# Seven block products for eight in the down projection of a two-layer encoder

## The chip, the cores and the metric

The kernel runs on one core of one Trainium2 chip. The metric is the device time of one execution in microseconds (us), lower being better. Five engines work side by side: TensorE (PE) multiplies, with its weight loads shown as PEld; VectorE (DVE), ScalarE (ACT) and GpSimd (POOL) work on elements; SyncE (SP) issues most of the transfers (DMA). TensorE writes its results into eight banks of PSUM, each 128 rows by 512 float32 columns.

## The reference, cut to what matters

Two encoder layers over 512 tokens of width 1024, each a token mixer with an output projection and then a SwiGLU feed-forward block with D_FF = 2816. Only the feed-forward block is touched:

```
def _swiglu(h, w_gate_up, w_down):
    gu = h @ w_gate_up
    g, u = gu[..., :D_FF], gu[..., D_FF:]
    return (jax.nn.silu(g) * u) @ w_down
...
x = x + _swiglu(_rmsnorm(x, norm_ffn[i]), w_gate_up[i], w_down[i])
```

The last product, the down projection, multiplies a 512 x 2816 activation by a 2816 x 1024 weight matrix and adds the result to x.

## The kernel before

**Products in three passes.** Every float32 operand is split into a rounded high part and the rest (`whi` and `wlo` for weights, `ah`/`al` or the two halves of an `op` tile for activations). `mm3` (lines 135 to 139) issues three matmuls for each product of a 128x128 block by a 128x512 block: high by high, high by low, low by high. `wsplit` (line 151) makes the split of a 128x1024 weight tile: ScalarE copies the high part (L154), VectorE subtracts (L155). `split` (line 248) does the same for activations (L249, L250).

**Gate and up projection** (`ffn`, line 784). These are already done with seven products for eight (`PROD`, line 781): the rows of the activation fall into two halves of 256 tokens, the inner dimension into two halves, and gate and up are the two column halves. Six groups `g` of columns each run the seven products. A product is cut into weight tiles (the `steps` list, line 833); `ahead` prepares the tiles up to `LW` = 2 steps before TensorE needs them. Sums of weight tiles are made partly by VectorE (lines 814, 821, 824) and partly by transfers that GpSimd issues and that add onto a tile already in SBUF (`dma_add`, line 806). The operand sums of the activation are built once, in group 0 (`sums`, line 709), and kept. The products gather in the pairs of banks A, B, C and D (`BANK`, line 919), and `post` (line 883) adds them up. The pool behind `whi` and `wlo` has three buffers of each (`WF` = 3), the pool of raw weight tiles three (`RF` = 3), and a general pool "G" 33 tiles of 128x1024. The pool "T" has nine tiles of 128x512.

**Down projection** (lines 949 to 1000). The activation stands transposed in eleven tiles `AT[kp]`, each with two of the 22 row blocks of the inner dimension for all 512 tokens. For each half `c` of the 1024 output columns, and each of the eleven `kp`, one weight tile is loaded and split, and 24 matmuls follow (four groups of 128 tokens, two row blocks, three passes). `split_a` (line 958) splits the activation tiles once, and both halves use the split. Four banks hold a half; `add_x` adds them to x (L686; in layer 1 line 998, after which line 999 writes the output). The transposes for the next layer (`emit(0)`, `emit(1)`) stand inside the second half and behind it, and `emit("weights")` loads the next layer's first two weight tiles early.

**Order of work.** The program text gives each engine's instructions a priority; a scheduler at build time fixes the order on each engine. On the chip every engine runs its own list in that order.

Of the kernel before, what the change touches and what calls it, by code (L numbers as in the profile page):

```python
# [18 lines left out]
P = 128  # L19
S = 512  # L20
D = 1024
# [27 lines left out]
def encoder_kernel(ctx: ExitStack, tc: tile.TileContext, a: dict, out: bass.AP):  # L49
# [14 lines left out]
    def wtile(dt, tag, bufs=None):  # L64
        return wpool[0][1].tile([P, wpool[0][2]], dt, tag=tag, name=nm(tag), **({"bufs": bufs} if bufs else {}))
# [10 lines left out]
    def g4(shape=(P, 1024), dt=F32R, name="g"):  # L76
        return gp_.tile(list(shape), dt, tag="G", name=nm(name))
# [25 lines left out]
    def bank(tag):  # L103
        return ps.tile([P, 512], F32, tag=tag, name=nm(tag), bufs=CFG[tag])

    def small(n, tag, dt=F32, bufs=4):
        return sp.tile([P, 1 if n == 1 else 16], dt, tag=tag, name=nm(tag), bufs=bufs)[:, :n]

    def f(ap):
        return ap.bitcast(F32)  # L110
# [32 lines left out]
    def eng(kind):  # L143
        c = cnt.get(kind, 0)
        cnt[kind] = c + 1
        p = CFG[kind]
        return p[c % len(p)]

    phase = ["s"]

    def wsplit(raw, n, kind):

        hi, lo = wtile(F32R, "whi"), wtile(F32R, "wlo")
        A.copy(hi[:, :n], raw)  # L154
        (V if eng(kind) == "V" else GP).tensor_sub(lo[:, :n], raw, f(hi[:, :n]))  # L155
        return hi, lo
# [12 lines left out]
    def load_w(src, n):  # L169
        return wsplit(load_raw(src, n)[:, :n], n, "wlo" + phase[0])  # L170
# [509 lines left out]
        transposes(tb, [X[t][:, k * P : (k + 1) * P] for t in range(4)])  # L680
        return tb

    def add_x(X, c, bs, sq, ts=range(4)):
        for t in ts:
            xc = X[t][:, c * 512 : (c + 1) * 512]
            V.tensor_add(xc, bs[t], xc)  # L686
            A.activation(tt(), xc, AF.Square, accum_out=sq[:, 4 * c + t : 4 * c + t + 1])

    def w_out(l, acts, banks, pre, X, g0, first, early):
# [94 lines left out]
    def ffn(l, X, acts, banks, pre, g0, emit):  # L784


        phase[0] = "f"
        NG = 6
        raws = {}
        ops = {}  # L790
        AT = {}
# [4 lines left out]
        def ntile(g):  # L796
            return 2 if g < 5 else 1
# [33 lines left out]
            return w  # L831

        steps = [(g, p, i) for g in range(NG) for p in PROD for i in range(ntile(g))]
        ready = {}
        nprep = [0]

        def ahead(n):
            while nprep[0] < min(n, len(steps)):
                g, p, i = steps[nprep[0]]
                if g == i == 0:  # L840
                    ops[p] = getop[0](AOP[p])
                if i == 0:
                    for q in {"P1": [1, 3], "P7": [2]}.get(p, []):
                        load_q(g, q)
                    if p == "P6":
                        load_q(g + 1, 0)
                    if p == "P3":
                        load_q(g + 1, 1)
                ready[g, p, i] = prep(g, p, i)
                nprep[0] += 1  # L850
# [22 lines left out]
        def act_T(g, act):  # L873
            n = width(g)
            for j in range(n // P):
                fb = 4 * g + j
                if fb % 2 == 0:
                    AT[fb // 2] = g4((P, 2, 512), F32, "at")
                tb = bank("tp")
                transposes(tb, [act[t][:, j * P : (j + 1) * P] for t in range(4)])  # L880
                A.copy(AT[fb // 2][:, fb % 2], tb)  # L881
# [35 lines left out]
                return [st["p1"][0], st["p1"][1], st["p5"][0], st["p5"][1]]  # L917

        BANK = dict(P1="A", P7="B", P2="A", P5="C", P6="D", P4="B", P3="C")
        pend = None  # L920
        s = 0
        for g in range(NG):
# [23 lines left out]
                    pend = None  # L946
            pend = act

        sq = small(8, f"sd{l}", bufs=1)
        ws = {}  # L950

        def load_d(c, kp):
            if kp < NF // 2:
                ws[c, kp] = load_w(a["w_dn"][l, c, kp], 1024)

        asp = {}

        def split_a(kp):
            if kp < NF // 2 and kp not in asp:
                hi, lo = g4(name="ah"), g4(name="al")  # L960
                x = AT[kp].rearrange("p a b -> p (a b)")
                A.copy(hi, x)
                (V if eng("wlod") == "V" else GP).tensor_sub(lo, x, f(hi))
                asp[kp] = (hi, lo)

        for kp in range(2):
            split_a(kp)
            load_d(0, kp)
        act_T(NG - 1, pend)
        for c in range(2):  # L970
            bs = [bank(x) for x in ("mm", "sc", "mm", "sc")]
            for kp in range(NF // 2):
                split_a(kp + 2)
                if (c, kp) not in ws:
                    load_d(c, kp)
                hi, lo = ws.pop((c, kp))
                ah, al = asp[kp]
                for t in range(4):
                    for j in range(2):
                        cs_ = slice(j * 512 + t * P, j * 512 + (t + 1) * P)  # L980
                        mm3(bs[t], (ah[:, cs_], al[:, cs_]), (hi[:, j * 512 : (j + 1) * 512], lo[:, j * 512 : (j + 1) * 512]),
                            kp == j == 0, kp == NF // 2 - 1 and j == 1)
                if c == 0 and kp + 2 < NF // 2 and (c, kp + 2) not in ws:
                    load_d(c, kp + 2)
                elif c == 1 and kp + 1 < NF // 2:
                    load_d(c, kp + 1)
                if c == 1 and kp == 2:
                    emit(0)
                if c == 1 and kp == NF // 2 - 2:
                    emit("weights")  # L990
            if c == 0:
                load_d(1, 0)
            if l == 0:
                add_x(X, c, bs, sq)
            else:
                for t in range(4):
                    xc = X[t][:, c * 512 : (c + 1) * 512]
                    V.tensor_add(xc, bs[t], xc)
                    nc.sync.dma_start(out[t * P : (t + 1) * P, c * 512 : (c + 1) * 512], xc)
        emit(1)  # L1000
        phase[0] = "a"
        if l == 0:
            tot = small(4, "sqt")
# [455 lines left out]
def _layout(i):  # L1459
    x, mem = i["x"][0], i["mem"][0]  # L1460
    arr = {}
    arr["xT"] = x.T.reshape(NK, P, S)
    arr["memT"] = _pk(np.ascontiguousarray(mem.T), NK)[0]
    qn, kn = i["mla_q_norm"][0], i["mla_k_norm"][0]
    arr["gains"] = np.concatenate(
        [_cols(i["mem_norm"]), _cols(i["norm_mix"][0]), _cols(i["norm_mix"][1]),
         _cols(i["norm_ffn"][0]), _cols(i["norm_ffn"][1]),
         i["memq_norm"].T, i["memk_norm"].T, _cols(qn[:P]), _cols(kn[:P]),
         _cols(i["mla_q_a_norm"][0]), _cols(i["mla_kv_a_norm"][0])], 1)
    gq, gk = i["gqa_q_norm"][0], i["gqa_k_norm"][0]  # L1470
# [13 lines left out]
    w = i["mla_w_kv_b"][0].reshape(256, 4, 2, 2, P)  # L1484
    arr["w_kvb"] = np.stack([_pk(w[:, g].transpose(0, 2, 1, 3).reshape(256, 512), 2)[0] for g in range(4)])
    w = i["w_mem_kv"]
    arr["w_mkv"] = np.stack([np.stack([_pk(w[l, :, c * 512 : (c + 1) * 512], NK)[0] for c in range(2)]) for l in range(2)])
    arr["x"] = x.reshape(4, P, D)
    w = i["w_out"]
    arr["w_out"] = w.reshape(2, 6, 2, P, 2, 512).transpose(0, 4, 1, 3, 2, 5).reshape(2, 2, 6, P, 1024)  # L1490
    w = i["w_gate_up"].reshape(2, 2, 4, P, 2, DFF)
    m = w[..., :2560].reshape(2, 2, 2, 2, P, 2, 5, 512)
    arr["w_gu"] = m.transpose(0, 6, 1, 5, 2, 4, 3, 7).reshape(2, 5, 4, 2, P, 1024)
    arr["w_gl"] = w[..., 2560:].transpose(0, 1, 4, 3, 2, 5).reshape(2, 4, P, 1024)
    w = i["w_down"].reshape(2, NF // 2, 2, P, 2, 512)
    arr["w_dn"] = w.transpose(0, 4, 1, 3, 2, 5).reshape(2, 2, NF // 2, P, 1024)
    w = i["gqa_w_in"][0]
    arr["w_gin"] = np.stack([_pk(w[:, c : c + 512], NK)[0] for c in (1024, 1536, 0, 512)])
    return {k: np.ascontiguousarray(v) for k, v in arr.items()}

# [18 lines left out]
```

## Time and profile before

| what | us |
|---|---|
| median of 3 runs | 1275.64 |
| lowest and highest | 1274.54, 1277.09 |
| the profiled execution, its own time | 1276.39 |
| its span in the trace | 1274.6 |

The times are device times of whole executions. The span runs from the first to the last instruction that the profiler recorded, and is a little shorter than the execution's own time. The down projection of layer 0 runs from about 538 to 661 us of the span, that of layer 1 from about 1150 us to the end.

### The profile page before, as it was taken

The page shows a single profiled execution, that of the slowest core. Times are in us where ns is not written, and L with a number is a line of the kernel's source. Part 1 is how long each engine was busy: PE and PEld are TensorE (multiplying, and loading weights), DVE is VectorE, ACT ScalarE, POOL GpSimd, SP SyncE. Part 2 cuts the span into 40 slices and gives each one's busy share as a digit, 9 for nine tenths or more (in the row PEclk, how much of TensorE's full clock was granted, in tenths as well). Part 3 has the DMA queues.
Part 4 walks back from the last instruction along what each step waited for, and adds up shares of the span by engine and source line. Part 5 has one row for each costly group of instructions (what it writes and reads, how often), then busy time and mean ns, then how long its engine had stood idle before and what let it go on. Part 6 is the DMA issues. An engine that isn't in the chain of part 4 may idle for free.

```text
span 1274.6 us, 17121 instructions
## 1 busy us (share of the span) xinstructions
PE 1262.3 (99%) x6425; PEld 1060.2 (83%) x6425; DVE 906.7 (71%) x1634; ACT 701.1 (55%) x1205; POOL 28.7 (2%) x43
## 2 busy tenths in 40 slices
PE   9999999999999999999999999999999999999998
PEld 7988878988778888988888888888877888898887
DVE  6699999745987887853336798965488897786222
ACT  6587766845655555542233578866475555555110
POOL 1000000001000000000000000000100000000000
PEclk9999999999999999999999999999999999999999
DMA  6342101056355433342223212213626534336210
GB/s 236 113 143 86 36 1 67 1 215 165 98 151 165 127 105 100 114 151 66 80 89 113 79 64 67 83 67 116 170 63 197 165 75 141 100 92 223 61 55 33
DMA packets 49202, 136.07 MB, mean 107 GB/s; under 512 B 5680, under 2 KB 10288, under 8 KB 49120
## 3 DMA queue, kind: packets, MB, share of 16 engines
q1 hardware_dynamic: 44784, 119.58, 27.2%
q0 software_dynamic: 4336, 15.40, 6.8%
q8 instruction: 50, 0.82, 0.3%
q14 instruction: 32, 0.26, 0.1%
HBM read 132.87 MB, written 2.10 MB: 106 GB/s over the span
## 4 chain that ended last, share of the span: by engine, by line
PE 94%; DVE 3%; ACT 2%; DMA 0%; issue 0%; SPq 0%
PE mm L138 15%; PE mm L139 15%; PE mm L137 15%; PE sc L138 13%; PE sc L137 13%; PE sc L139 13%; PE tp L347 6%; PE sc L500 4%; DVE wlo L155 1%; ACT whi L154 1%; PE tp L566 1%; DMA raw<-in_w_cin 0%; ACT t L888 0%; DVE g L246 0%; ACT at L881 0%
## 5 line engine op out<-in xcount | busy, mean ns | idle before, releaser
L155 DVE TENSOR_TENSOR wlo<-raw,whi 128x1024 fp32r<-128x1024 f32 (+3 forms) x342 | 344.2, 1012 | 248.9 <-ACT whi L154 246.1
L154 ACT CAST whi<-raw 128x1024 fp32r<-128x1024 f32 (+3 forms) x342 | 300.7, 885 | 387.5 <-PE sc L139 290.2
L137 PE MATMUL mm<-whi,g 128*128 128x512 f32 (+3 forms) x370 | 141.4, 383 | 0.0
L138 PE MATMUL mm<-wlo,g 128*128 128x512 f32 (+3 forms) x370 | 139.0, 376 | 0.0
L139 PE MATMUL mm<-whi,g 128*128 128x512 f32 (+3 forms) x370 | 138.2, 377 | 0.0
L138 PE MATMUL mm<-wlo,op 128*128 128x512 f32 (+1 forms) x336 | 126.0, 375 | 3.3 <-DVE wlo L155 3.3
L137 PE MATMUL mm<-whi,op 128*128 128x512 f32 (+1 forms) x336 | 126.1, 375 | 0.3
L139 PE MATMUL mm<-whi,op 128*128 128x512 f32 (+1 forms) x336 | 125.2, 373 | 0.0
L138 PE MATMUL sc<-wlo,op 128*128 128x512 f32 (+1 forms) x336 | 124.9, 372 | 0.0
L137 PE MATMUL sc<-whi,op 128*128 128x512 f32 (+1 forms) x336 | 124.9, 372 | 0.0
L139 PE MATMUL sc<-whi,op 128*128 128x512 f32 (+1 forms) x336 | 124.9, 372 | 0.0
L137 PEld LDWEIGHTS mm<-whi,g 128*128 128x128 f32 x370 | 69.6, 188 | 10.4 <-ACT g L243 0.7
L139 PEld LDWEIGHTS mm<-whi,g 128*128 128x128 f32 x370 | 69.4, 188 | 10.6 <-DVE g L246 0.2
L138 PEld LDWEIGHTS mm<-wlo,g 128*128 128x128 f32 x370 | 69.7, 188 | 9.4
L138 PEld LDWEIGHTS mm<-wlo,op 128*128 128x128 f32 x336 | 63.3, 188 | 16.3 <-DVE wlo L155 5.9
L500 PE MATMUL sc<-g,g 128*128 128x512 f32 x256 | 73.9, 407 | 0.3 <-ACT g L243 0.3
L137 PEld LDWEIGHTS mm<-whi,op 128*128 128x128 f32 x336 | 63.3, 188 | 11.4 <-ACT whi L154 0.8
L139 PEld LDWEIGHTS sc<-whi,op 128*128 128x128 f32 x336 | 63.3, 188 | 11.0
L138 PEld LDWEIGHTS sc<-wlo,op 128*128 128x128 f32 x336 | 63.3, 188 | 11.0
L137 PEld LDWEIGHTS sc<-whi,op 128*128 128x128 f32 x336 | 63.3, 188 | 10.9
L139 PEld LDWEIGHTS mm<-whi,op 128*128 128x128 f32 x336 | 63.3, 188 | 10.4
L138 PE MATMUL sc<-wlo,ah 128*128 128x512 f32 x176 | 68.7, 391 | 0.0
(251 smaller groups left out, 2566.5 us busy)
## 6 DMA issues: line engine op xcount, KB each, us to landing
raw<-in_w_gu SPq DMA_DIRECT2D x80, 512.0 KB, 4.4
raw<-in_w_dn SPq DMA_DIRECT2D x44, 512.0 KB, 4.3
raw<-in_w_gu POOLq DMA_DIRECT2D x24, 512.0 KB, 5.3
raw<-in_w_out SPq DMA_DIRECT2D x22, 512.0 KB, 4.5
raw<-in_w_mkv SPq DMA_DIRECT2D x32, 256.0 KB, 2.8
raw<-in_w_gin SPq DMA_DIRECT2D x30, 256.0 KB, 3.0
raw<-in_w_gl SPq DMA_DIRECT2D x8, 512.0 KB, 4.0
raw<-in_w_out SPq DMA_DIRECT2D x12, 256.0 KB, 2.5
```

The source lines that it names most:

```text
L137: PE.matmul(out, lhi, rhi, start=start, stop=False, skip_group_check=skip)
L138: PE.matmul(out, lhi, rlo, start=False, stop=False, skip_group_check=skip)
L139: PE.matmul(out, llo, rhi, start=False, stop=stop, skip_group_check=skip)
L154: A.copy(hi[:, :n], raw)
L155: (V if eng(kind) == "V" else GP).tensor_sub(lo[:, :n], raw, f(hi[:, :n]))
L347: PE.transpose(dst[:, i * P : (i + 1) * P], s, ident)
L500: PE.matmul(sc, lq[:, q * P : (q + 1) * P], rk, start=i == 0, stop=i == len(passes) - 1)
L566: PE.transpose(tb4[:, k, j, :], self.p[j][:, k * P : (k + 1) * P], ident)
```

## The change

In each layer the first 16 of the 22 row blocks of the down projection (`KS` = 4 weight tiles in each of two halves of the inner dimension) are done with seven products for eight: token halves, inner halves and the two column halves `c` are the 2x2 blocks. The other six row blocks (three `kp`) are multiplied as before, by 24 matmuls for each half and `kp`, and gather in the same banks: A and B hold half 0, C and D hold half 1 with the opposite sign, so that the plain weights of half 1 are split negated and `add_x` subtracts there. Half 1 is finished first. All eight banks are held to the end of the stage.

The weight sums come from transfers: four tiles "t0" (half 0) take three additions each in turn, between the products P1, P5, P6 and P4, and four tiles "t3" (half 1) take one before P7. All 16 are issued by GpSimd. The activation operands are built for each weight tile anew, a 128x512 sum on VectorE for P7, P5, P6 and P3, and a split for all seven. P1 and P7 are copied out of PSUM (`post_down`), P5 and P6 are added to these copies, and six more VectorE operations put the copies into x. The last two transposes of the activation (`act_T(NG - 1, pend)`) move behind P1. The order of `emit` is turned: 1 inside the last part, 0 at the end; the rows of the weight `w_gin` are swapped to suit.

```
-    def wsplit(raw, n, kind):
+    def wsplit(raw, n, kind, neg=False):
         hi, lo = wtile(F32R, "whi"), wtile(F32R, "wlo")
+        if neg:
+            A.mul(hi[:, :n], raw, -1.0)
+            V.scalar_tensor_tensor(lo[:, :n], raw, -1.0, f(hi[:, :n]), ALU.mult, ALU.subtract)
+            return hi, lo
...
         steps = [(g, p, i) for g in range(NG) for p in PROD for i in range(ntile(g))]
+        steps += [("d", p, i) for p in PROD for i in range(4)] + [("d", c, k) for c in (1, 0) for k in range(2 * KS, NF // 2)]
...
                 g, p, i = steps[nprep[0]]
+                if g == NG - 1 and p in ("P6", "P4"):
+                    down_loads(p)
+                if g == "d":
+                    ready[g, p, i] = prep_down(p, i)
...
+        def down_loads(p):
+            for i in range(KS):
+                k = ("t0" if p == "P6" else "t3", i)
+                if k not in dn:
+                    dn[k] = w_dn(0 if p == "P6" else 1, i, g4(dt=F32, name="raw"))
+                    if p == "P4":
+                        GP.dma_start(dn[k], a["w_dn"][l, 1, KS + i], accum_op=ALU.add)
+
+        def prep_down(p, i):
+            if p in (0, 1):
+                w = wsplit(load_raw(a["w_dn"][l, p, i], 1024), 1024, "wlof", p == 1)
+                if i not in asp:
+                    asp[i] = g4(name="ah"), g4(name="al")
+                    split(asp[i], AT[i].rearrange("p a b -> p (a b)"))
+                return w, asp[i]
+            (a11, a21), (a12, a22) = [[AT[k][:, :, h * 256 : (h + 1) * 256] for h in range(2)] for k in (i, KS + i)]
...
+            if p in ("P2", "P3"):
+                raw = load_raw(a["w_dn"][l, int(p == "P3"), KS + i], 1024)
+            else:
+                raw = dn["t3" if p == "P7" else "t0", i]
+            if p == "P7":
+                x = new()
+                V.tensor_sub(x, a11, a21)
+            elif p == "P5":
+                x = dn["s", i] = new()
+                V.tensor_sub(x, a22, a21)
+            elif p in ("P6", "P3"):
+                x = dn["s", i]
+                V.scalar_tensor_tensor(x, x, -1.0, a11 if p == "P6" else a12, ALU.mult, ALU.subtract)
+            else:
+                x = dict(P1=a11, P2=a12, P4=a22)[p]
+            o = g4((P, 2, 2, 256), name="op")
+            split((o[:, 0], o[:, 1]), x)
+            w = wsplit(raw, 1024, "wlof")
+            if p in ("P1", "P5", "P6"):
+                c, k = dict(P1=(1, i), P5=(1, KS + i), P6=(0, KS + i))[p]
+                GP.dma_start(raw, a["w_dn"][l, c, k], accum_op=ALU.add)
+            return w, o
+
+        def post_down(p):
+            if p in ("P1", "P7"):
+                st[p] = two()
+                for t in range(2):
+                    A.copy(st[p][t], st[BANK[p]][t])
+            for t in range(2):
+                w, z = st["P1"][t], (st["P7"][t] if p != "P1" else None)
+                if p == "P5":
+                    V.tensor_add(z, st["C"][t], z)
+                    V.tensor_add(z, z, w)
+                elif p == "P6":
+                    V.tensor_add(w, st["D"][t], w)
...
+        for p in PROD:
...
+            for i in range(KS):
+                ahead(s + 1 + CFG["LW"])
+                (hi, lo), o = ready.pop(("d", p, i))
+                for j in range(2):
+                    for t in range(2):
...
+                        mm3(st[bk][t], lh, (hi[:, j * 512 : (j + 1) * 512], lo[:, j * 512 : (j + 1) * 512]),
+                            first and i == j == 0, i == KS - 1 and j == 1, skip=p in ("P2", "P4", "P3"))
+                s += 1
+            post_down(p)
+            if p == "P1":
+                act_T(NG - 1, pend)
...
-        for c in range(2):
-            bs = [bank(x) for x in ("mm", "sc", "mm", "sc")]
-            for kp in range(NF // 2):
...
+        for c in (1, 0):
+            bs = st["C"] + st["D"] if c else st["A"] + st["B"]
+            for kp in range(2 * KS, NF // 2):
+                ahead(s + 1 + CFG["LW"])
+                (hi, lo), (ah, al) = ready.pop(("d", c, kp))
...
+                if c and kp == 2 * KS:
...
+                    for t in range(2):
+                        w, z = st["P1"][t], st["P7"][t]
+                        V.tensor_sub(X[t][:, 512:], X[t][:, 512:], w)
+                        V.tensor_sub(X[2 + t][:, 512:], X[2 + t][:, 512:], z)
+                        V.tensor_add(X[2 + t][:, :512], X[2 + t][:, :512], w)
                     emit("weights")
-            if c == 0:
-                load_d(1, 0)
+                if c == 0 and kp == NF // 2 - 2:
+                    emit(1)
             if l == 0:
-                add_x(X, c, bs, sq)
+                add_x(X, c, bs, sq, neg=c == 1)
...
-        emit(1)
+        emit(0)
```

## Rows read from the trace of the kernel before

**Rows 1.** The page: busy time of each engine, its share, its instructions.
```profile
PE 1262.3 (99%) x6425; PEld 1060.2 (83%) x6425; DVE 906.7 (71%) x1634; ACT 701.1 (55%) x1205; POOL 28.7 (2%) x43
```

**Rows 2.** Windows: stretch, its length, busy time by engine, granted clock, DMA share.
```profile
core 0: us, PE busy (x) PEld busy (x) DVE busy (x) ACT busy (x) POOL busy (x), PEclk, DMA share, GB/s
340.00:360.00 20.00, 18.86 (x84) 14.98 (x83) 19.45 (x25) 9.37 (x12) 1.71 (x2) 1.00 0.73 199
425.00:465.00 40.00, 39.94 (x185) 33.00 (x184) 31.77 (x35) 21.34 (x26) 1.72 (x2) 1.00 0.46 131
505.00:545.00 40.00, 39.92 (x268) 36.55 (x267) 33.50 (x44) 23.67 (x33) 0.86 (x1) 1.00 0.41 132
545.00:600.00 55.00, 55.00 (x244) 45.53 (x243) 23.95 (x23) 19.59 (x24) 0.00 (x0) 1.00 0.27 91
600.00:661.00 61.00, 61.00 (x279) 50.35 (x278) 17.21 (x18) 15.05 (x23) 2.18 (x4) 1.00 0.23 75
```

**Rows 3.** Timeline of TensorE, end of layer 1: first and last of 71.
```profile
1254.64 0.39 PE L138 MATMUL mm<-wlo,ah 128*128 128x512 f32 x1
...
1270.50 0.39 PE L139 MATMUL sc<-whi,al 128*128 128x512 f32 x1
```

**Rows 4.** Instructions that read `ah`: one of six like forms (min/median/max ns).
```profile
L137 PE MATMUL mm<-whi,ah x176: 387/389/476, 538.2 to 1268.7; 128*128 128x512 f32 x176
```

**Rows 5.** VectorE by shape, 330 to 680 us: busy us, mean ns, idle before.
```profile
L155 DVE TENSOR_TENSOR wlo<-raw,whi 128x1024 fp32r<-128x1024 f32 x92 | 111.7, 1221 | 87.3 <-ACT whi L154 86.1 <-PE tp L347 0.7
...
L905 DVE TENSOR_TENSOR t<-t,t 128x512 f32<-128x512 f32 x10 | 6.6, 683 | 0.0
...
L250 DVE TENSOR_TENSOR op<-hs,op 128x512 fp32r<-128x512 f32 x4 | 2.7, 685 | 0.1
...
L717 DVE SCALAR_TENSOR_TENSOR hs<-hs,hr 128x512 f32<-128x512 f32 x2 | 1.4, 681 | 0.0
```

**Rows 6.** ScalarE by shape, the same stretch.
```profile
L154 ACT CAST whi<-raw 128x1024 fp32r<-128x1024 f32 x91 | 95.7, 1054 | 136.0 <-PE sc L139 111.9 <-DVE raw L824 13.6 <-issue 3.3
...
L249 ACT CAST op<-hs 128x512 fp32r<-128x512 f32 x3 | 1.8, 621 | 0.3 <-DVE hs L717 0.3
```

**Rows 7.** Timeline of VectorE in groups 0 and 1: start, length.
```profile
336.86 0.68 DVE L900 TENSOR_TENSOR t<-mm,t 128x512 f32<-128x512 f32 x1
337.46 0.68 DVE L900 TENSOR_TENSOR t<-sc,t 128x512 f32<-128x512 f32 x1
338.06 0.68 DVE L250 TENSOR_TENSOR op<-hr,op 128x512 fp32r<-128x512 f32 x1
...
358.41 2.35 DVE L814 TENSOR_TENSOR raw<-raw,raw 128x1024 f32<-128x1024 f32 x2
...
371.30 1.23 DVE L821 TENSOR_TENSOR raw<-raw,raw 128x1024 f32<-128x1024 f32 x1
372.45 1.22 DVE L155 TENSOR_TENSOR wlo<-raw,whi 128x1024 fp32r<-128x1024 f32 x1
373.58 1.22 DVE L814 TENSOR_TENSOR raw<-raw,raw 128x1024 f32<-128x1024 f32 x1
374.72 1.22 DVE L821 TENSOR_TENSOR raw<-raw,raw 128x1024 f32<-128x1024 f32 x1
```

**Rows 8.** Waits of the weight loads, 335 to 385 us: us, times, longest.
```profile
PEld mm L138 <- DVE wlo L155: 2.9, 3, 1.2
PEld mm L137 <- ACT whi L154: 0.4, 1, 0.4
```

**Rows 9.** Line 808, the adding transfers of GpSimd (ns; landing in us).
```profile
L808 POOL DMA_DIRECT2D raw<-in_w_gu x24: 848/858/1195, 293.7 to 1088.6; - x24
...
DMA to landing us min/median/max: 5.1/5.3/9.8
```

**Rows 10.** Timeline of GpSimd, 900 to 930 us.
```profile
913.97 1.75 POOL L808 DMA_DIRECT2D raw<-in_w_gu  x2 [8.75 <-DMA raw<-in_w_gu]
921.51 0.85 POOL L808 DMA_DIRECT2D raw<-in_w_gu  x1 [5.79 <-DVE wlo L155]
```

**Rows 11.** Line 808, the two of 914 us alone.
```profile
L808 POOL DMA_DIRECT2D raw<-in_w_gu x2: 862/1028/1195, 914.0 to 914.5; - x2
...
DMA to landing us min/median/max: 6.2/8.0/9.8
```

**Rows 12.** Windows around two such transfers, columns as in the second group.
```profile
473.00:482.00 9.00, 9.00 (x46) 7.53 (x44) 8.19 (x10) 4.37 (x6) 1.72 (x2) 1.00 0.73 124
```

**Rows 13.** The page: queue of the plain loads, packets, MB, share.
```profile
q1 hardware_dynamic: 44784, 119.58, 27.2%
```

**Rows 14.** Timeline of VectorE, the kernel's last instruction there.
```profile
1270.93 0.69 DVE L998 TENSOR_TENSOR x<-sc,x 128x512 f32<-128x512 f32 x1 [0.67 <-PE sc L139]
```

More of the change, by code (lines that the diff above doesn't have):

```diff
@@ L681, in x_T, with add_x @@
         return tb
-    def add_x(X, c, bs, sq, ts=range(4)):
+    def add_x(X, c, bs, sq, ts=range(4), neg=False):
         for t in ts:
             xc = X[t][:, c * 512 : (c + 1) * 512]
-            V.tensor_add(xc, bs[t], xc)
+            if neg:
+                V.tensor_sub(xc, xc, bs[t])
+            else:
+                V.tensor_add(xc, bs[t], xc)
             A.activation(tt(), xc, AF.Square, accum_out=sq[:, 4 * c + t : 4 * c + t + 1])
@@ L787, in ffn @@
         phase[0] = "f"
-        NG = 6
+        NG, KS = 6, 4
         raws = {}
@@ L839, in ahead @@
                 g, p, i = steps[nprep[0]]
+                if g == NG - 1 and p in ("P6", "P4"):
+                    down_loads(p)
+                if g == "d":
+                    ready[g, p, i] = prep_down(p, i)
+                    nprep[0] += 1
+                    continue
                 if g == i == 0:
@@ L919, in ffn, with w_dn @@
         BANK = dict(P1="A", P7="B", P2="A", P5="C", P6="D", P4="B", P3="C")
+        dn = {}
+        asp = {}
+        def w_dn(c, kp, dst):
+            nc.sync.dma_start(dst, a["w_dn"][l, c, kp])
+            return dst
+        def down_loads(p):
[5 more added lines that the diff above has]
+                        GP.dma_start(dn[k], a["w_dn"][l, 1, KS + i], accum_op=ALU.add)
@@ new lines, in prep_down, with new @@
+        def prep_down(p, i):
[6 more added lines that the diff above has]
+            (a11, a21), (a12, a22) = [[AT[k][:, :, h * 256 : (h + 1) * 256] for h in range(2)] for k in (i, KS + i)]
+            def new():
+                return tt().rearrange("p (a b) -> p a b", a=2)
+            if p in ("P2", "P3"):
[11 more added lines that the diff above has]
+                V.scalar_tensor_tensor(x, x, -1.0, a11 if p == "P6" else a12, ALU.mult, ALU.subtract)
+            else:
+                x = dict(P1=a11, P2=a12, P4=a22)[p]
[6 more added lines that the diff above has]
+            return w, o
@@ L947, in ffn @@
             pend = act
-        sq = small(8, f"sd{l}", bufs=1)
[L950 to L969, printed above, removed]
-        for c in range(2):
-            bs = [bank(x) for x in ("mm", "sc", "mm", "sc")]
-            for kp in range(NF // 2):
[L973 to L977, printed above, removed]
+        for p in PROD:
+            bk = BANK[p]
+            first = p in ("P1", "P7", "P5", "P6")
+            if first:
+                st[bk] = [bank(x) for x in (("tp", "tp") if bk == "D" else ("mm", "sc"))]
+            for i in range(KS):
[3 more added lines that the diff above has]
+                    for t in range(2):
+                        lh = o[:, 0, j, t * P : (t + 1) * P], o[:, 1, j, t * P : (t + 1) * P]
+                        mm3(st[bk][t], lh, (hi[:, j * 512 : (j + 1) * 512], lo[:, j * 512 : (j + 1) * 512]),
[4 more added lines that the diff above has]
+                act_T(NG - 1, pend)
+        sq = small(8, f"sd{l}", bufs=1)
+        for c in (1, 0):
[3 more added lines that the diff above has]
+                (hi, lo), (ah, al) = ready.pop(("d", c, kp))
                 for t in range(4):
@@ L981, in ffn @@
                         mm3(bs[t], (ah[:, cs_], al[:, cs_]), (hi[:, j * 512 : (j + 1) * 512], lo[:, j * 512 : (j + 1) * 512]),
[L982 to L989, printed above, removed]
+                            False, kp == NF // 2 - 1 and j == 1, skip=True)
+                s += 1
+                if c and kp == 2 * KS:
[4 more added lines that the diff above has]
+                        V.tensor_add(X[2 + t][:, :512], X[2 + t][:, :512], w)
                     emit("weights")
-            if c == 0:
-                load_d(1, 0)
+                if c == 0 and kp == NF // 2 - 2:
+                    emit(1)
             if l == 0:
-                add_x(X, c, bs, sq)
+                add_x(X, c, bs, sq, neg=c == 1)
             else:
@@ L997, in ffn @@
                     xc = X[t][:, c * 512 : (c + 1) * 512]
-                    V.tensor_add(xc, bs[t], xc)
+                    if c:
+                        V.tensor_sub(xc, xc, bs[t])
+                    else:
+                        V.tensor_add(xc, bs[t], xc)
                     nc.sync.dma_start(out[t * P : (t + 1) * P, c * 512 : (c + 1) * 512], xc)
-        emit(1)
+        emit(0)
         phase[0] = "a"
@@ L1497, in _layout @@
     w = i["gqa_w_in"][0]
+    w = np.concatenate([w[512:], w[:512]])
     arr["w_gin"] = np.stack([_pk(w[:, c : c + 512], NK)[0] for c in (1024, 1536, 0, 512)])
```

## The prediction

> **What bounds the kernel now.** The page comes first [rows 1]. TensorE is busy 99% of the span, VectorE 71%, ScalarE 55%. As a busy TensorE need not be one that is never kept waiting, the windows come second [rows 2]: in the gate and up projection it is busy 39.94 of 40 us, in the down projection 55.00 of 55 and 61.00 of 61, and its granted clock is 1.00 everywhere, the upper of its two levels, 2.4 GHz. Third is the timeline, for the true price of a matmul [rows 3]: a row shows 0.39 us, but rows overlap. From the first start to the last, 70 matmuls later, 15.86 us pass: 0.2266 us for one. That pitch, not 0.39, is what a matmul less gives back. So the down projection is a solid row of matmuls. Nothing can be gained there but by issuing fewer, and everything else that the change adds must stay behind those that are left.
>
> **What is removed.** The down projection has six forms of 176 matmuls like the one shown [rows 4], 1056 in all, 528 for each layer. After the change the first 16 row blocks take 7 products x 4 weight tiles x 12 matmuls = 336, the other six 3 x 2 x 24 = 144: 480 for each layer. 48 fewer in each of two layers, 96 x 0.2266 = **21.75 us**. A product's tile has the same 128x512 matmuls as in the gate and up projection, so I see no reason for another pitch.
>
> Moving the last two transposes behind P1 gives nothing: TensorE lost only 0.08 us between 505 and 545 us [rows 2], where they stood. The end of the kernel stays as it is: four last additions of the same size, then the output [rows 14].
>
> **What is added on VectorE and ScalarE.** Below, a block is one weight tile's step: 12 matmuls, 12 x 0.2266 = 2.72 us of TensorE. VectorE rows overlap too: 128x512 operations start 0.60 us apart, 128x1024 ones 1.14 us [rows 7]. A block of P1, P2 or P4 needs a weight subtraction (1.14) and an operand subtraction (0.60): 1.74 us. One of P7, P5, P6 or P3 also the operand sum: 2.34 us. For a layer that is 12 x 1.74 + 16 x 2.34 = 58.3, and six bank additions of 0.60 make 61.9 us, against 28 x 2.72 = 76.2 us of TensorE: 81%. The nearest row is a whole group of the gate and up projection, with VectorE busy 31.77 of 40 us, 79%, and TensorE losing 0.06 us [rows 2]. ScalarE needs at most 1.05 + 0.62 us for a block [rows 6], well below 2.72. So this work is hidden, if it comes in a good order. The denser stretch bounds it from above: from 340 to 360 us, where operands are built as well as weight sums, VectorE is busy 97% and TensorE loses 1.14 us; in all the weight loads of that region waited 2.9 + 0.4 = 3.3 us [rows 2, 8]. There a block asks 1.14 x 2 + 0.60 x 2 = 3.5 us of VectorE, more than 2.72; here none does. Between 0 and 3.3 us for each layer I take 0.5, **1.0 us** for both, near the steady row. The six plain weight tiles, the three split activation tiles and the six additions to x come in steps of 24 matmuls, 5.4 us each: hidden, as VectorE was busy 24 of 55 us in the old stage [rows 2].
>
> **What is added on the queues.** The plain loads stay 22 for each layer, but 16 adding transfers of 512 KB are new. GpSimd takes 0.86 us to issue one, and it lands 5.3 us after the issue (5.1 to 9.8) [rows 9]. The two of 914 us landed at 914.0 + 6.2 and 914.5 + 9.8, so 4.1 us apart [rows 10, 11]. Two others, from 473 to 482 us, made 0.73 x 9 = 6.6 us of all transfer engines, some of it plain loads: at most 3.3 us each [rows 12]. So a queue of them advances by one in S = 3.3 to 4.1 us, and TensorE eats a block in 2.72. The additions before P7 and P5 have time: those for P7 are called for eight blocks ahead, some 20 us, those after P1 have eight blocks (P7 and P2), 21.8 us. The tight place is P5, P6, P4: eight additions in a row, each of which must land before the same tile's next split, four blocks on.
>
> I count from TensorE's start of P5's first block. With three buffers of `whi`, a split can begin two blocks ahead of use, at -5.44, and takes 1.05 + 1.22 us [rows 5, 6], 2.4 with the hand-overs. The first addition is issued at -3.0 and lands at 2.3; the eighth lands at 2.3 + 7 x S. P4's last block then is ready 2.4 us later, and due at 11 x 2.72 = 29.9. With S = 3.3 it is ready at 27.8, in time; with 3.7 at 30.6, 0.7 late; with 4.1 at 33.4, 3.5 late. I take 3.7, the middle, since a plain load can run beside: **1.4 us** for both layers.
>
> The Trainium skill ("SBUF — State Buffer", section "SBUF: two separate sides") speaks against these transfers: one issued from GpSimd can starve for descriptors while VectorE runs an operation that takes the port pair the two engines share. The rows do not show that here: VectorE was busy 8.19 of 9.00 us while GpSimd issued two in 0.86 us each [rows 12]. By the rule each would wait for a VectorE operation, and the sum would be that of rival 3; by the row it stands.
>
> **The sum.** Against the profiled execution's own 1276.39 us: 1276.39 - 21.75 + 1.0 + 1.4 = 1257.0. That execution lies 0.75 us above the median of the three runs, 1275.64, so I forecast **1256.3 us**.
>
> **The rivals.**
>
> *1. The chain of adding transfers is late.* S = 4.1 and nothing else: 2 x 3.5 = 7 us, so 1275.6 - 21.8 + 1.0 + 7 = 1262. If P3's four plain loads also fall among them, each adds 0.524 / 119.58 x 0.272 x 1274.6 = 1.5 us [rows 13], 6 for a layer: 1274. For it speaks the pair of 914 us; against it, that plain loads need only a free raw buffer and can run early, and that the same pair had plain loads beside it.
>
> *2. VectorE falls behind in the blocks with sums.* At the price of the dense stretch, 3.3 us for each layer: 1253.9 + 6.6 + 1.4 = 1262. Against it: 2.34 us is below 2.72.
>
> *3. Every adding transfer waits for one more VectorE operation*, 1.22 us [rows 5], so S = 3.7 + 1.2 = 4.9: 2.3 + 34.3 + 2.4 - 29.9 = 9.1 late for each layer, 1253.9 + 18.2 + 1.0 = 1273. The Trainium skill's rule above is its ground; the issue times speak against it.
>
> *4. Slower: VectorE and ScalarE hand a block back and forth.* If each engine works strictly block by block, a block with a sum takes 0.68 (sum) + 0.62 (operand copy) + 1.05 (weight copy) + 1.22 (weight subtraction) = 3.57 us [rows 5, 6], 0.85 more than TensorE's. 16 blocks x 0.85 + 3.6 (bank additions) = 17.2 us for each layer, with 10.9 gained: 1275.6 + 2 x 6.3 = 1288. It decides from (10.9 - 3.6) / 16 = 0.46 us lost per block. Against it speaks the order on VectorE: at 373.58 us the sum of line 814, which serves P7 of group 2, ran between the two sums of line 821 for P6 of group 1 [rows 7], four products ahead of its turn. What is ready is drawn forward, and so would the next block's sum be.
>
> *5. No change*: only if late weights cost just what the matmuls give, the upper end of 1 or 3.
>
> **How the numbers follow.** The forecast as a case (no matmul pitch lost, up to 5 us of waits, 1253.5 to 1259) has a chance of 0.70; rival 1 0.13, rival 2 0.06, rival 3 0.03, rival 4 0.06, rival 5 0.02. The range runs from 1253 (all of 21.75 and a little scatter; the three runs lay 1.4 us around their median) to 1265, which takes in rival 2 and the first half of rival 1: some 0.84. A difference below 0.2%, 2.6 us, is about what a measurement here cannot tell from none. Faster by more: 0.70 + 0.06 and nearly all of 1 and 3, 0.91; within it 0.03; slower 0.06.
>
> **What would show it.** Right: 960 matmuls in the two down projections at a pitch of 0.2266 us, each stage near 109 us where it was 120, the granted clock at 1.00, TensorE without a wait above 0.5 us; VectorE some 80% busy in the seven products. Step 1 (queue) is wrong if weight loads in P6 or P4 wait for `whi` and that for an adding transfer. Step 2 (VectorE) is wrong if they wait for `wlo` or the operand's low half while no transfer is late. Rival 4 would show as VectorE idle behind ScalarE in every block. What would make the whole wrong: a longer pitch, or a clock that falls to 1.2 GHz in waits.

## The result, and the profile after

| | median us | lowest to highest | ratio to before, 95% interval |
|---|---|---|---|
| before, 4 runs beside | 1276.37 | 1274.54 to 1277.72 | 1 |
| changed | 1257.31 | 1256.18 to 1260.12 | 0.9855 (0.9834 to 0.9876) |

Forecast were 1256.3 us and a range of 1253 to 1265. The kernel is 19.1 us faster, where the count of matmuls alone gives 21.75.

The page of the changed kernel, busy time by engine, the queue of GpSimd's transfers and the issues. These answer to [rows 1, 9, 13].

```profile
PE 1242.1 (99%) x6329; PEld 1042.5 (83%) x6329; DVE 981.5 (78%) x1754; ACT 743.6 (59%) x1277; POOL 56.4 (4%) x75
...
q1 hardware_dynamic: 44784, 119.58, 27.5%
q0 software_dynamic: 8944, 32.18, 13.8%
...
raw<-in_w_dn POOLq DMA_DIRECT2D x32, 512.0 KB, 9.8
raw<-in_w_gu POOLq DMA_DIRECT2D x24, 512.0 KB, 5.4
```

6425 - 6329 = 96 matmuls fewer, as counted. The plain loads are the same 119.58 MB. The 32 new additions take 9.8 us to land in the median, while the old ones of the gate and up weights still take 5.4: the same operation, of the same size, is slower where it stands close to others and beside plain loads.

The windows of the changed kernel: the gate and up projection, then the down projection of layer 0 in three parts; columns as in the second group of rows ahead of the prediction.

```profile
425.00:465.00 40.00, 39.94 (x185) 33.01 (x184) 31.75 (x35) 21.45 (x26) 1.72 (x2) 1.00 0.46 132
...
541.00:576.00 35.00, 35.00 (x163) 29.15 (x162) 31.58 (x44) 23.04 (x32) 4.03 (x5) 1.00 0.68 169
576.00:606.00 30.00, 29.86 (x130) 23.80 (x128) 26.43 (x35) 17.85 (x25) 5.46 (x7) 1.00 0.90 207
606.00:655.00 49.00, 48.60 (x221) 39.65 (x221) 26.33 (x32) 18.71 (x29) 2.18 (x4) 1.00 0.22 71
```

Gate and up are as before [rows 2]. In the down projection the clock stays at its upper level, and TensorE loses time only where the transfer engines are 90% busy, and just behind it. (A matmul's row is longer than its pitch, so a short wait hardly shows in these windows; the waits themselves follow below.)

For an account of the stage I take its length from the timeline of TensorE: from its first 128x512 matmul behind the 128x256 ones of group 5 to the next layer's first matmul (layer 0), or to its own last one (layer 1). The kernel before:

```profile
538.16 0.40 PE L137 MATMUL mm<-whi,ah 128*128 128x512 f32 x1
...
661.40 0.47 PE L137 MATMUL mm<-t,g 128*128 128x512 f32 x1
...
1150.06 0.40 PE L137 MATMUL mm<-whi,ah 128*128 128x512 f32 x1
```

and the changed kernel:

```profile
541.45 0.40 PE L137 MATMUL mm<-whi,op 128*128 128x512 f32 x1
...
655.55 0.47 PE L137 MATMUL mm<-t,g 128*128 128x512 f32 x1
...
1144.11 0.40 PE L137 MATMUL mm<-whi,op 128*128 128x512 f32 x1
...
1254.03 0.39 PE L139 MATMUL sc<-whi,al 128*128 128x512 f32 x1
```

With the end of layer 1 before [rows 3], layer 0 takes 114.10 us for 123.24, layer 1 109.92 for 120.44: 9.14 + 10.52 = 19.66 us gained in the two stages, 2.1 less than the count. The profiled execution as a whole gained less, 1276.39 - 1260.12 = 16.3 us. Its stage of layer 0 begins 3.3 us later than before; that comes from the first 16 us of the kernel, which the change does not touch (last section).

What is missing stands in the waits of the weight loads (us, times, longest) of the changed kernel, first layer 0, 541 to 655 us, then layer 1, 1144 to 1254 us.

```profile
PEld mm L138 <- DVE wlo L159: 2.2, 4, 0.8
...
PEld mm L138 <- DVE wlo L159: 0.5, 1, 0.5
```

The four of layer 0 follow each other by about a block. P5's first block starts at 574.79 us (four blocks before P6, whose first matmul is the first into the banks `tp`, at 585.89). Counted from there in blocks of 2.72 us, the four fall into P4's second, third and fourth block and P3's first (timeline of the weight loads; the bracket is the idle time before, and what ended it):

```profile
574.79 0.19 PEld L137 LDWEIGHTS mm<-whi,op 128*128 128x128 f32 x1
...
600.01 0.19 PEld L138 LDWEIGHTS mm<-wlo,op 128*128 128x128 f32 x1 [0.56 <-DVE wlo L159]
603.04 0.19 PEld L138 LDWEIGHTS mm<-wlo,op 128*128 128x128 f32 x1 [0.42 <-DVE wlo L159]
606.13 0.19 PEld L138 LDWEIGHTS mm<-wlo,op 128*128 128x128 f32 x1 [0.48 <-DVE wlo L159]
609.53 0.19 PEld L138 LDWEIGHTS mm<-wlo,op 128*128 128x128 f32 x1 [0.77 <-DVE wlo L159]
```

VectorE is named, but in P4 it is only the last link. The timeline of ScalarE shows for whom the high part waited, for the second and third of these waits:

```profile
600.67 1.05 ACT L158 CAST whi<-raw 128x1024 fp32r<-128x1024 f32 x1 [1.97 <-DMA raw<-in_w_dn]
603.77 1.05 ACT L158 CAST whi<-raw 128x1024 fp32r<-128x1024 f32 x1 [2.04 <-DMA raw<-in_w_dn]
```

A transfer, and no other: ScalarE sat idle 2 us before each. For the first of the four the addition landed at 588.0 + 9.4 = 597.4 us, and the copy followed at 597.66.

The fourth wait, at P3's first block, has another last link. Its weights are a plain load. ScalarE and VectorE, both held up until then, first split two activation tiles of the plain part (`ah`, `al`), and the `wlo` that TensorE waits for comes behind them:

```profile
604.73 1.99 ACT L253 CAST ah<-at 128x1024 fp32r<-128x1024 f32 x2
...
606.00 2.35 DVE L254 TENSOR_TENSOR al<-at,ah 128x1024 fp32r<-128x1024 f32 x2
608.27 1.21 DVE L159 TENSOR_TENSOR wlo<-raw,whi 128x1024 fp32r<-128x1024 f32 x1
```

The only wait of layer 1 falls on the same block (P4 starts there at 1199.2 us, so P3 at 1210.1):

```profile
1210.80 0.19 PEld L138 LDWEIGHTS mm<-wlo,op 128*128 128x128 f32 x1 [0.52 <-DVE wlo L159]
```

So half of the 2.7 us of waits, 0.77 + 0.52, reaches TensorE through the order of work on ScalarE and VectorE. The experiments below take away both kinds together; none separates them.

The eight additions of P5 and P6 in layer 0 are issued from 572.87 to 593.84 us (timeline of GpSimd); line 981 gives the landing times, here of the first and of the eighth alone.

```profile
L981 POOL DMA_DIRECT2D raw<-in_w_dn x1: 857/857/857, 572.9 to 572.9; - x1
...
DMA to landing us min/median/max: 7.4/7.4/7.4
...
L981 POOL DMA_DIRECT2D raw<-in_w_dn x1: 865/865/865, 593.8 to 593.8; - x1
...
DMA to landing us min/median/max: 9.8/9.8/9.8
```

So they land from 580.3 to 603.6 us, (603.6 - 580.3) / 7 = 3.3 us apart, where TensorE takes a block in 2.72. The queue of the additions from 572 to 604 us (packets, MB, share of 16 engines):

```profile
q0 software_dynamic: 1152, 4.19, 68.5%
```

That is these eight and no other, so each took 0.685 x 32 / 8 = 2.7 us of the transfer engines, as much as a block of TensorE; plain loads come on top.

### The profile page after: what moved, and what is told of

The parts are those of the page before. It is cut to its first block, busy times and chain, and to the rows that moved or that the text cites. A ratio compares the mean times of both kernels' runs of the same rounds, so it can differ in the third digit from the quotient of the medians.

```text
span 1258.1 us, 17244 instructions
## 1 busy us (share of the span) xinstructions
PE 1242.1 (99%) x6329; PEld 1042.5 (83%) x6329; DVE 981.5 (78%) x1754; ACT 743.6 (59%) x1277; POOL 56.4 (4%) x75
## 3 DMA queue, kind: packets, MB, share of 16 engines
q1 hardware_dynamic: 44784, 119.58, 27.5%
## 4 chain that ended last, share of the span: by engine, by line
PE 91%; DVE 4%; ACT 2%; DMA 1%; issue 1%; SPq 0%; POOL 0%; ACTq 0%; POOLq 0%
PE mm L138 14%; PE mm L139 14%; PE mm L137 14%; PE sc L138 12%; PE sc L137 12%; PE sc L139 12%; PE tp L351 6%; PE sc L504 4%; DVE wlo L159 1%; ACT whi L158 1%; DMA raw<-in_w_dn 1%; PE tp L137 1%; PE tp L139 1%; PE tp L138 1%; DMA raw<-in_w_cin 1%
## 5 line engine op out<-in xcount | busy, mean ns | idle before, releaser
L158 ACT CAST whi<-raw 128x1024 fp32r<-128x1024 f32 (+3 forms) x360 | 319.5, 894 | 322.2 <-PE sc L139 190.9
L159 DVE TENSOR_TENSOR wlo<-raw,whi 128x1024 fp32r<-128x1024 f32 (+3 forms) x360 | 365.7, 1021 | 163.5 <-ACT whi L158 160.6
L138 PE MATMUL mm<-wlo,op 128*128 128x512 f32 (+1 forms) x432 | 164.0, 380 | 4.0 <-DVE wlo L159 3.7
L137 PE MATMUL mm<-whi,op 128*128 128x512 f32 (+1 forms) x432 | 163.6, 379 | 0.3 <-ACT whi L158 0.2
L139 PE MATMUL mm<-whi,op 128*128 128x512 f32 (+1 forms) x432 | 162.6, 376 | 0.0
L138 PE MATMUL sc<-wlo,op 128*128 128x512 f32 (+1 forms) x432 | 162.3, 376 | 0.0
L137 PE MATMUL sc<-whi,op 128*128 128x512 f32 (+1 forms) x432 | 162.3, 376 | 0.0
L139 PE MATMUL sc<-whi,op 128*128 128x512 f32 (+1 forms) x432 | 162.2, 376 | 0.0
L138 PEld LDWEIGHTS mm<-wlo,op 128*128 128x128 f32 x432 | 81.3, 188 | 22.5 <-DVE wlo L159 8.6
L137 PEld LDWEIGHTS mm<-whi,op 128*128 128x128 f32 x432 | 81.3, 188 | 15.1 <-ACT whi L158 0.8
L139 PEld LDWEIGHTS sc<-whi,op 128*128 128x128 f32 x432 | 81.3, 188 | 14.8
L137 PEld LDWEIGHTS sc<-whi,op 128*128 128x128 f32 x432 | 81.3, 188 | 14.7
L139 PEld LDWEIGHTS mm<-whi,op 128*128 128x128 f32 x432 | 81.4, 188 | 14.0
L815 POOL DMA_DIRECT2D raw<-in_w_gu x24 | 20.7, 862 | 883.0 <-DMA raw<-in_w_gu 544.4
```

Source lines behind the costliest of these rows:

```text
L137: PE.matmul(out, lhi, rhi, start=start, stop=False, skip_group_check=skip)
L138: PE.matmul(out, lhi, rlo, start=False, stop=False, skip_group_check=skip)
L139: PE.matmul(out, llo, rhi, start=False, stop=stop, skip_group_check=skip)
L815: GP.dma_start(raws[g, q][i], w_src(g, by)[i], accum_op=ALU.add)
```

## The experiments

Two questions: is it the additions or VectorE that costs the 2 us, and if it is the additions, is it their number, or the short time between two uses of a tile? The stage lengths are read as above; "waits" are those of weight loads for `whi` or `wlo` in the stage.

| kernel | median us | ratio (95%) | layer 0 | layer 1 | waits, both layers |
|---|---|---|---|---|---|
| before | | | 123.24 | 120.44 | 0 |
| changed | 1257.31 | 0.9855 (0.9834 to 0.9876) | 114.10 | 109.92 | 2.7 |
| changed, again | 1257.44 | 0.9839 (0.9820 to 0.9858) | 113.75 | 110.42 | 3.0 |
| no additions behind P5, P6 | 1254.34 | 0.9822 (0.9806 to 0.9838) | 112.30 | 109.50 | 0 |
| no operand sums | 1259.36 | 0.9857 (0.9843 to 0.9872) | 116.68 | 110.30 | 4.0 |
| spread order | 1253.69 | 0.9813 (0.9799 to 0.9828) | 112.31 | 109.50 | 0 |
| 20 of 22, spread order | 1249.91 | 0.9785 (0.9770 to 0.9799) | 108.38 | 106.77 | 0 |
| 8 of 22 | 1274.68 | 0.9980 (0.9970 to 0.9990) | 121.97 | 118.57 | 8.9 |
| 20 of 22, old order | 1248.48 | 0.9764 (0.9750 to 0.9779) | 108.42 | 106.81 | 0 |
| no plain loads for P3 | 1255.57 | 0.9826 (0.9809 to 0.9844) | 112.32 | 109.50 | 0 |

Each ratio is to runs of the kernel before on the same chip in the same call (medians 1276.37, 1277.82 and 1277.20). Layer 0 with 20 of 22 ends its stage before the last transposes, so only its layer 1 compares exactly. The waits of 8 of 22 take in 1.1 us at the first tile of the plain part in layer 0 (`wlo` of line 156), which is not a t0 tile. The expectations reckon layer 0's stage some 0.8 us shorter than this table (113.3 us for the changed kernel); what is to be compared is the differences.

**The changed kernel again.** 

> The changed kernel again, beside the others of this call on one chip: ratio 0.985 to 0.986, down stages near 113 and 110 us, a loss of 1 to 2.5 us for both layers against the stages without waits.

It repeats, with a ratio of 0.9839, a little below what was expected: 2.4 us lost against the stages without waits, (113.75 - 112.31) + (110.42 - 109.50).

**No additions behind P5 and P6.**

```
-            if p in ("P1", "P5", "P6"):
+            if p == "P1":
                 c, k = dict(P1=(1, i), P5=(1, KS + i), P6=(0, KS + i))[p]
                 GP.dma_start(raw, a["w_dn"][l, c, k], accum_op=ALU.add)
```

> The eight adding transfers behind P5 and P6 are left out in each layer (so P6 and P4 multiply weights that lack these addends). Theory A (the chain P5, P6, P4 of adding transfers makes the last weights late, which cost 1.75 of the 10.88 us of layer 0): the waits of P4's weight loads for wlo go, the down stage of layer 0 falls from 113.3 to about 111.6 us, that of layer 1 stays within 0.4 of 109.9, and the time is some 2 us below the changed kernel's 1257.3: 1255.5. Theory B (VectorE is behind in the blocks with sums): the stage of layer 0 stays at 113.3 and the time at 1257.

No wait for `whi` or `wlo` is left, and the stages fall to 112.30 and 109.50 us. All of VectorE's work is still there. Layer 0 falls by 1.8 us, where 1.7 were expected. Theory A holds.

**No operand sums.**

```
-            if p == "P7":
-                x = new()
-                V.tensor_sub(x, a11, a21)
...
-            else:
-                x = dict(P1=a11, P2=a12, P4=a22)[p]
+            x = dict(P1=a11, P7=a21, P2=a12, P5=a21, P6=a11, P4=a22, P3=a12)[p]
```

> The operand sums on VectorE for P7, P5, P6 and P3 are left out (the products multiply a plain quarter of the activation instead of a sum); all transfers stay. Theory A (adding transfers): nothing changes, layer 0 stage 113 us, time 1257 within 1. Theory B (VectorE): 16 x 0.60 = 9.6 us less of VectorE for each layer, the waits for wlo go, layer 0 stage 111.6, time 1255.5.

Theory B is out: with 9.6 us less on VectorE in each layer the stage of layer 0 is 2.6 us longer, not shorter, and in layer 1, which has no next layer's weights to prepare, waits remain (1.0 us; the stage takes 110.30 us for 109.92). But Theory A's number missed too. Timeline of ScalarE in layer 0:

```profile
579.82 1.05 ACT L158 CAST whi<-raw 128x1024 fp32r<-128x1024 f32 x1 [1.67 <-DMA raw<-in_w_dn]
586.78 0.62 ACT L253 CAST t<-t 128x512 fp32r<-128x512 f32 x1 [5.91 <-DMA t<-in_w_gin]
587.30 1.99 ACT L158 CAST whi<-raw 128x1024 fp32r<-128x1024 f32 x2
```

and the weight loads there:

```profile
588.39 0.19 PEld L137 LDWEIGHTS tp<-whi,op 128*128 128x128 f32 x1 [1.87 <-ACT whi L158]
589.65 0.19 PEld L138 LDWEIGHTS tp<-wlo,op 128*128 128x128 f32 x1 [1.07 <-DVE wlo L159]
```

The copy of a weight of the *next* layer (`w_early`, called by `emit("weights")`) stands before two urgent copies of `whi` in ScalarE's list, and waits 5.9 us for its load. It is the second of two such copies; in the changed kernel the first comes at 592.19 us without a wait, and the second not before 617.12 us, with a wait of 0.97 us. That the build drew it forward because the sums had left tiles of pool T free is argued, not shown. What is shown is that one early copy in an engine's list holds up all behind it.

**The spread order.**

```
+    DPROD = ["P1", "P7", "P5", "P2", "P6", "P3", "P4"]
...
-        for p in PROD:
+        for p in DPROD:
```

(also in the list of steps). 

> Only the order of the seven products in the down projection is changed: P1, P7, P5, P2, P6, P3, P4 in place of P1, P7, P2, P5, P6, P4, P3, so that every addition onto a t0 tile has eight blocks (21.8 us) before its next use where two of three had four (10.9 us). Theory A: no wait for wlo or whi in the stage, layer 0 at 111.6 us, layer 1 at 109.6, time 1255.5. Theory B (VectorE): the same number of VectorE operations in the same stage, no gain: 1257. If the additions' total load on the transfer engines and not their place in a chain is the matter: no gain either, the waits only move.

No wait for `whi` or `wlo` is left, with all 32 additions and all sums in place. Start and end of the two stages:

```profile
536.53 0.40 PE L137 MATMUL mm<-whi,op 128*128 128x512 f32 x1
...
648.84 0.47 PE L137 MATMUL mm<-t,g 128*128 128x512 f32 x1
...
1137.27 0.40 PE L137 MATMUL mm<-whi,op 128*128 128x512 f32 x1
...
1246.77 0.39 PE L139 MATMUL sc<-whi,al 128*128 128x512 f32 x1
```

Windows of layer 0, and the landing of all 24 additions onto t0 tiles in both layers (line 982 there):

```profile
572.00:602.00 30.00, 30.00 (x134) 24.86 (x133) 30.00 (x38) 20.40 (x25) 3.45 (x4) 1.00 0.84 234
```
```profile
L982 POOL DMA_DIRECT2D raw<-in_w_dn x24: 860/867/869, 533.7 to 1187.3; - x24
...
DMA to landing us min/median/max: 5.4/7.0/9.9
```

VectorE is busy 30.00 of 30 us in the hardest stretch and TensorE still loses nothing, so VectorE's load was not the matter. (Its rows overlap, as the prediction says, so 30.00 does not mean that nothing more would fit in.) The additions land faster, too, 7.0 us in the median where the changed kernel's take 9.3, as a product without additions lies between two with them. The stages, 112.31 and 109.50 us, gain (123.24 - 112.31) + (120.44 - 109.50) = 21.87 us: the count's 21.75, whole.

**8 of 22 row blocks (KS = 2).**

```
-        NG, KS = 6, 4
+        NG, KS = 6, 2
```

(and `range(KS)` in the list of steps). 

> KS = 2 in the changed kernel's own order: 8 of the 22 row blocks by seven products. By the count 24 matmuls fewer for each layer, 48 x 0.2266 = 10.9 us. Theory A1 (the chain's length in time decides: what is added behind a product must land before the same tile comes again, KS blocks on): with two blocks, 5.4 us, against a landing of 5.3 to 10 us, it is 2 to 4 us late for each layer, waits for whi and wlo in P6 and P4, ratio 0.995 to 0.998 (4 to 7 us gained). Theory A2 (the load of the additions, half as many, decides): no waits, 10.9 us gained, ratio 0.9915.

Half the matmuls are saved, with half the additions, and nearly all of the gain is gone: 0.9980. The stages by the count would be 123.24 - 24 x 0.2266 = 117.80 and 115.00; they are 121.97 and 118.57, 4.2 and 3.6 us late. Of layer 0's 4.2 us, about 1.1 us are the wait for line 156 named above, which layer 1 does not have. Else TensorE waits in P6 and hardest at P4's first block (weight loads, layer 0):

```profile
568.82 0.19 PEld L137 LDWEIGHTS mm<-whi,op 128*128 128x128 f32 x1 [2.06 <-ACT whi L158]
570.08 0.19 PEld L138 LDWEIGHTS mm<-wlo,op 128*128 128x128 f32 x1 [1.07 <-DVE wlo L159]
```

The additions themselves are quicker than in the changed kernel (line 981, both layers), so it is not their load:

```profile
L981 POOL DMA_DIRECT2D raw<-in_w_dn x12: 860/864/867, 535.9 to 1175.3; - x12
...
DMA to landing us min/median/max: 5.3/5.7/7.4
```

A landing of 5.7 us and a split of 2.3 us do not fit into two blocks of 2.72. Theory A1 holds, at the upper end of its 2 to 4 us for each layer.

**20 of 22 row blocks, spread and old order (KS = 5).** Both as KS = 4, with

```
-        NG, KS = 6, 4
+        NG, KS = 6, 5
...
-                if c == 0 and kp == NF // 2 - 2:
+                if c == 0 and kp == NF // 2 - 1:
                     emit(1)
```

> As the spread order, and KS = 5: 20 of the 22 row blocks go by seven products, two plainly (the transposes for the next layer's half 1 are called behind the last plain tile, since there is only one for each half). By the count, 7 x 5 x 12 + 2 x 24 = 468 matmuls for each layer, 12 fewer than with KS = 4: 24 x 0.2266 = 5.4 us less than the spread order, 1250. Rival: the 33 tiles of pool G and the nine of pool T, fuller by three to four tiles, hold loads and sums back at the entry of the stage, and it gives 1253 or more.

> KS = 5 in the changed kernel's own order of products. Theory A1 (time between two uses of a tile): five blocks, 13.6 us; the tenth addition lands at 5.1 + 9 x 3.33 = 35.1 and its weights are ready at 37.5, due at 14 x 2.72 = 38.1: hardly late, ratio 0.979 as with the spread order. Theory A2 (load): ten additions in a row for eight, so more loss than the 2.2 us of KS = 4: 3 us or more above the spread order's stages, ratio 0.981 or above.

Both give the same stages, without a wait for weights: layer 1 in 106.77 and 106.81 us, where the count gives 109.50 - 12 x 0.2266 = 106.78. Windows of layer 0 in the old order:

```profile
540.00:640.00 100.00, 100.00 (x447) 82.90 (x446) 84.51 (x107) 58.51 (x81) 11.23 (x13) 1.00 0.64 147
```

More additions in a row, and the old order, and no loss: a fifth block between two uses of a tile is enough, though the additions of line 981 take 9.9 us to land in the median there, and up to 17.8 (behind P1, where they have ten blocks). The rival of too few tiles is out as well. These two are the fastest, 1248.5 and 1249.9 us; 28 us below the kernel before and some 8 below the change as made. Which of the two is faster the runs cannot tell.

**No plain loads for P3.**

```
-            if p in ("P2", "P3"):
-                raw = load_raw(a["w_dn"][l, int(p == "P3"), KS + i], 1024)
+            if p == "P2":
+                raw = load_raw(a["w_dn"][l, 0, KS + i], 1024)
             else:
-                raw = dn["t3" if p == "P7" else "t0", i]
+                raw = dn["t3" if p in ("P7", "P3") else "t0", i]
```

> The four plain loads of P3 are left out (P3 multiplies the tiles of P7 again), so that hardly a plain load runs beside the additions of P5 and P6; all 16 additions and all of VectorE's work stay. If the additions alone advance by 3.3 us each, the waits of P4 stay, the stages as in the changed kernel. If the plain loads beside them are what makes them late (some 1.5 us each, four in that stretch in layer 0), the waits go: stages 111.6 and 109.5 us as in the spread order, ratio 0.982.

The waits go. Line 981 from 565 to 592 us, the eight additions of P5 and P6 in layer 0:

```profile
L981 POOL DMA_DIRECT2D raw<-in_w_dn x8: 860/864/867, 569.4 to 588.2; - x8
...
DMA to landing us min/median/max: 5.4/7.1/9.7
```

and the same eight of the changed kernel, 570 to 594.5 us:

```profile
L981 POOL DMA_DIRECT2D raw<-in_w_dn x8: 857/862/865, 572.9 to 593.8; - x8
...
DMA to landing us min/median/max: 7.4/9.8/10.5
```

The eight additions are not alone, though that was expected. With P3's loads gone the plain part's are called earlier, and three run beside the later additions; in the changed kernel it is five, from before the first addition on (line 170, 569 to 598 us here, then 571 to 600 us of the changed kernel):

```profile
L170 SPq DMA_DIRECT2D raw<-in_w_dn x3: 328/328/328, 579.9 to 590.8; - x3
...
L170 SPq DMA_DIRECT2D raw<-in_w_dn x5: 327/328/328, 571.5 to 594.8; - x5
```

So the first addition lands 5.4 us after its issue and not 7.4, and the last 588.2 + 9.7 - 538.0 = 59.9 us into the stage and not 593.8 + 9.8 - 541.4 = 62.2. They still land 3.3 us apart, (597.9 - 574.8) / 7, though issued 2.7 apart. The run shows that two loads fewer, and none beside the first additions, are enough for the chain to come in time; what eight additions alone would do it does not show. The Trainium skill ("DMA: Bandwidth & Descriptors", section "Queues, rings and completion order") says that each transfer engine takes turns, packet by packet, between the queues that have work for it. The trace is in keeping with it: the additions are slower with loads beside them, and the transfer engines were 1.05 busy from 582 to 585 us. The turns themselves were not read from it.

## Why the prediction was right

**The count** was exact: 96 matmuls, 21.75 us forecast, 21.87 in the stages of the spread order, which differs in the order of products alone.

**The pitch and the clock** did not change, and nothing else of the stage came onto TensorE's path: the transposes, the copies out of PSUM and the six additions to x are hidden, as the stages without waits equal the count.

**VectorE** was forecast at 1.0 us, and its amount of work cost nothing. The waits name it, but removing its sums shortened nothing, and with the spread order it is 100% busy for 30 us without loss. The term should have been 0; the bound of 3.3 us came from a stretch that asked more than TensorE's block time, and was rightly not taken. What the prediction called hidden, the split of the plain part's activation tiles, did take part in a wait: drawn forward into P4, it stood before P3's first weights once the additions were late.

**The chain of additions** was named in its place, P5, P6, P4, and its size was near: 1.4 us forecast, (114.10 - 112.31) + (109.92 - 109.50) = 2.2 us found, 2.4 in the second profile. Three numbers inside it were off and in part made up for each other. S was 3.3 us, the lower bound, not 3.7. But in layer 0 the first addition was issued 1.9 us before P5's first block, not 3.0 (572.87 against 574.79), and it landed 7.4 us after its issue, not 5.3, with plain loads beside it: the "plain load among them" that I had put into rival 1 was the case, at a smaller price than there. With these, the sum gives 5.5 + 7 x 3.3 + 2.4 - 29.9 = 1.1 us for P4's last block; the three waits in P4 add up to 0.56 + 0.42 + 0.48 = 1.46. The wait at P3's first block stood in no term.

That the total of what was added came out, 1.0 + 1.4 = 2.4 forecast for 2.2 to 2.4 found, is in part luck: a term that should have been 0 stood beside one that was too small.

**The rivals.** Rival 1's mechanism is thus the true one behind what was lost, at 2.2 and not 7 us. Rival 2 and 3 did not occur: GpSimd's issues of the eight additions took 0.86 us each, and S was 3.3, not 4.9. The port rule of the Trainium skill ("SBUF — State Buffer", "SBUF: two separate sides") is about VectorE operations that take the port pair; the prediction drew waits from it without asking whether the operations of this kernel do. In the spread order none of the 24 issues of line 982 took more than 0.869 us, and the best landing was 5.4 us, with VectorE at 30.00 of 30 in the hardest stretch. With the operations of this kernel such waits did not occur; the runs have no operation that would show the rule itself at work. Rival 4, the slower one, needs VectorE to idle in every block; it was busy 31.58 of 35 us. A copy drawn forward at the wrong place did hold ScalarE up in one experiment, though, a danger that I had not listed.

What the prediction did not draw from its own sum is how the loss changes with the number of blocks. With S = 3.7 the same sum has P4's last block 2.3 + 3 x 3.7 + 2.4 - 5 x 2.72 = 2.2 us late for KS = 2, 0.7 for KS = 4, and in time for KS = 5: 2.3 + 9 x 3.7 + 2.4 - 14 x 2.72 = -0.1. The direction is right. The saving nearly vanished with KS = 2 and came whole with KS = 5.

## What to carry to other kernels

Where TensorE is solidly busy, a saved matmul gives back its pitch (here 0.2266 us, from first to last start), and the rest of the working goes into what must be ready in time. For a buffer that is added to in place between uses, compare two times: issue to landing plus the split behind it (here 5.3 us in the median of the kernel before, 7.4 to 10.5 us in the chain of layer 0, plus 2.3 us), against the work that lies between two uses; lengthen the second by putting unrelated products between, or by larger products, before trying to shorten the first. A wait that names an engine is followed back: in P4 `wlo` waited for `whi`, and `whi` for a transfer. An engine that works through a list in order can also hand a delay on to work that did not wait for the transfer, as at P3's first block.

## What the runs showed of the hardware

An adding transfer of 512 KB landed 5.3 us after its issue in the median of the kernel before. In the chain of layer 0, with the transfer engines 90% busy, each took 7.4 to 10.5 us, while one landed every 3.3 us; with fewer plain loads beside them (no plain loads for P3) each took 5.4 to 9.7 us, and still one landed every 3.3 us.

The first 16 us of the kernel vary by some 4 us without any change there. Windows of 8 to 16 us, before and then changed:

```profile
8.00:16.00 8.00, 7.95 (x35) 6.06 (x34) 6.62 (x13) 7.14 (x15) 0.00 (x0) 1.00 1.03 374
```
```profile
8.00:16.00 8.00, 5.28 (x18) 3.93 (x17) 5.01 (x9) 5.53 (x12) 0.00 (x0) 0.79 0.92 316
```

The first loads land later (ScalarE waits 3.6 us for a tile of the input, where it was 2.3), TensorE idles (one wait of 2.7 us for `whi`), and the granted clock of the stretch is 0.79: for some 3 us behind the wait TensorE runs in part at the lower level, 1.2 GHz. By 16 us TensorE has begun 37 matmuls where it had begun 50; 13 x 0.2266 = 2.9 of the 3.3 us. Both profiles of the changed kernel had it; the profiles of the spread order (clock 1.00 in this stretch) and of the other experiments did not, and the down projection is far off at that time. Among the executions of the kernel before, those with a mean clock of 0.997 had spans of 1277.3 to 1278.1 us, those with 1.000 of 1274.0 and 1274.1; that they differ by the same start is argued, as only the profiled ones show it. Such a start can hide or feign a change of 0.3%; the stage lengths are free of it.
